# Gate/up of an fp32 encoder block: which operand of the matmul stands and which moves

## Chip, cores and metric

One NeuronCore of a Trainium2 chip runs the whole kernel in one launch. The metric is the device time of one execution in microseconds (us). A kernel is timed in several runs, and the median is given with the lowest and the highest. The profile is one further execution, taken by the hardware profiler.

TensorE (PE) multiplies: a stationary tile of 128x128 is loaded first (PEld in the profile), then a moving tile of up to 512 columns streams past it, and the sums land in PSUM, which has 8 banks of 128x512 fp32. VectorE (DVE), ScalarE (ACT) and GpSimd (POOL) do the elementwise work. SyncE (SP) issues the transfers from and to DRAM. Each engine works through its own instructions in the order in which the program lists them, and waits where a tile is not there yet or not yet free.

## Reference

An encoder block over 512 tokens of width 2048, in fp32: a projection, two attention mixers of 8 heads, an output projection with a residual, and a SwiGLU feed-forward of width 5632.

```python
mixed = jnp.concatenate([out_a, out_b], axis=-1)
x = x + jnp.einsum('bse,ed->bsd', mixed, w_out[layer])
h2 = rmsnorm(x, g_ffn[layer])
gate, up = jnp.split(jnp.einsum('bsd,df->bsf', h2, w_gate_up[layer]), 2, axis=-1)
x = x + jnp.einsum('bsf,fd->bsd', jax.nn.silu(gate) * up, w_down[layer])
return rmsnorm(x, g_final)
```

## The kernel before

**Numbers.** Each fp32 operand is split into a high part (ACT copies it rounded) and a low part (DVE subtracts the high part). `mm3` (L170) makes one product of three matmuls: high by high, high by low, low by high (L172 to L174).

**Stages on TensorE.** Input projection and attention run to about 610 us, the output projection (PSUM tiles `pw`) to 720, gate/up (`gu`) to 1610, down (`dn` plain, `st` in Strassen form) to 2036, and the last down tiles (`fd`) with the final norm to the end. The output projection has two rounds of four chunks of 512 columns, kinds A and B. After each B chunk, DVE adds the residual (L570), and `h_side` (L624) transposes two pairs of 128-row tiles of the new x (`x1t`, L629); `pair_forms` (L596) makes the forms of a pair.

**Strassen-like forms.** Gate/up multiplies 2x2 blocks in seven products, m1 to m7. On the token side `pair_forms` makes four differences of 256 columns (`ta`, `tb`, L601) and splits them, in the pieces m1, b2, ta and tb, ACT and DVE by turns. There are eight pairs, `hf[0]` to `hf[7]`, and four more for each of the three down sets. On the weight side `Form.weights` (L668) makes sums of weight blocks (`m`, L676), and `split_hi` (L698, ACT at L702) and `split_lo` (L212, DVE) give the tiles `fw`.

**Gate/up.** 44 groups (`Group`, L707), one for each f-tile of 128. A group has seven forms by two halves of the 2048 rows; each is a unit of 12 matmuls with a weight tile stationary and 256 columns of a token form moving. The result has f on the partitions. `chain_step` (L739) copies or adds the forms' results out of PSUM as soon as each is done, DVE multiplies by the norm's factor, spread over partitions by `spread_r2` (L643) into `r2b`, ACT applies silu (L764), and the product `up` is stored to DRAM as one act tile. The first group (`post`, L785) runs all forms of half 0, then all of half 1. Down reads the act tiles back.

**Order.** The program writes every engine's order by hand, over a list `units` with estimated durations. Before unit n, `prepare(n)` (L1048) issues the raw loads that are due within `LOAD_AHEAD` (24 us of estimated time) as far as one of the four raw buffers of 1 MB is free, the loads of side inputs within `SIDE_AHEAD` (13), and the high parts of weights within `SPLIT_AHEAD` (10), each low part one unit after its high part. Then the unit's matmuls follow, and one entry of the `side` queue is taken: an eviction, a transposition, a step of attention. All working tiles are slots of one pool of 80 (`N_SLOTS`).

Of the kernel before, what the change touches and what calls it, by code (L numbers as in the profile page):

```python
# [19 lines left out]
P = 128  # L20
# [23 lines left out]
LAST_WAIT = 2  # L44
PLAIN_WAIT = 5
DOWN_PLAIN = (8, 4, 4)
# [9 lines left out]
def encoder_block(ctx, tc, x, g_mix, w_in, g_q_a, g_k_a, g_out_a, g_out_b, w_out, g_ffn,  # L56
# [3 lines left out]
    wp = ctx.enter_context(tc.tile_pool(name="wstream", bufs=1))  # L60
    dp = ctx.enter_context(tc.tile_pool(name="spill", bufs=1, space=bass.MemoryType.DRAM))
    sp = ctx.enter_context(tc.tile_pool(name="slots", bufs=1))
# [10 lines left out]
    def slot(base, dtype=F32, shape=(P, 512)):  # L73
        return sp.tile(list(shape), dtype, tag="s", bufs=N_SLOTS, name=nm(base))

# [21 lines left out]
    r2b = cp.tile([P, S], F32, name="r2b")  # L97
# [60 lines left out]
    def split(src, name, gain=None, between=None):  # L158
        hi, lo = slot(name + "h", F32R), slot(name + "l", F32R)
        if gain is None:  # L160
            nc.scalar.activation(hi, src, AF.Copy)
            nc.vector.tensor_tensor(lo, src, f32(hi), op=OP.subtract)
# [18 lines left out]
    class Raw:  # L181
        def __init__(self, pieces, first=False):
            self.pieces, self.first, self.t = pieces, first, None

        def load(self):
            if self.t is None:
                self.t = wp.tile([P, 4 * 512], F32, tag="raw", bufs=N_RAW, name=nm("raw"))
# [8 lines left out]
    class Unit:  # L196
        dur = UNIT_US

        def __init__(self, raw, sub, mm, post=None, early=None, side_in=None):
            self.raw, self.sub, self.mm, self.post = raw, sub, mm, post  # L200
            self.early, self.side_in = early, side_in or []
# [15 lines left out]
    side = deque()  # L217

# [6 lines left out]
    def x_transposes(k):  # L225
# [3 lines left out]
        if k == 0:  # L229
            xT[k] = split(ps, "xT", gm[:, k:k + 1])  # L230
            nc.scalar.activation(ssx, ps, AF.Square)
        else:
            sq = slot("xsq")
            xT[k] = split(ps, "xT", gm[:, k:k + 1], lambda: nc.scalar.activation(sq, ps, AF.Square))
# [69 lines left out]
    def post_kvA(ps):  # L304
        for j in range(2):
            vA[j] = (slot("vh", F32R, (P, 2, 256)), slot("vl", F32R, (P, 2, 256)))
# [15 lines left out]
    def transpose_k_a(kv):  # L322
# [3 lines left out]
        kTA[kv] = split(ps, "kT")  # L326
# [11 lines left out]
    def post_vB(j, ps):  # L338
        for t in range(NT):
            r = r1["r"][:, t:t + 1]  # L340
            h, l = slot("vbh", F32R), slot("vbl", F32R)
# [26 lines left out]
    H = {}  # L368
    oT = {}
    acc = {}  # L370
    heads = []

    class Head:
# [126 lines left out]
    def add_chunk(w, rows, pieces, mm, post, early=None, side_in=None, dur=UNIT_US):  # L500
        for j in range(0, len(rows), 4):
# [6 lines left out]
            for s in range(m):  # L508
# [3 lines left out]
                units[-1].dur = dur  # L512

    def in_chunk(pieces, post):
# [7 lines left out]
        add_chunk(w_in, [k * P for k in range(KD)], pieces, mm, lambda: post(box["ps"]))  # L522
# [23 lines left out]
    def out_chunk(kind, c):  # L546
# [3 lines left out]
        def early(k):  # L550
            if (kind, k) not in oS:
                drain_until(lambda: (kind, k) in oT)
                oS[kind, k] = split(oT.pop((kind, k)), "oS", go[:, base + k:base + k + 1])

        def mm(u, k):
            if k == 0:
                box["ps"] = [bank("pw") for _ in range(NT)]
                if kind == "A":
                    x1[c] = [slot("x1") for _ in range(NT)]
# [5 lines left out]
        def post():  # L565
# [9 lines left out]
            if kind == "B":  # L575
# [7 lines left out]
                if c == NC - 1:  # L583
                    side.append(spread_r2)
        add_chunk(w_out, [(base + k) * P for k in range(NHA)], [(c * 512, 0, 512)], mm, post, early)
# [8 lines left out]
    m1_pair = []  # L594

    def pair_forms(a, b, kind, n):  # L596
        ta, tb = slot("ta"), slot("tb")
        left, right = slice(0, 256), slice(256, 512)
# [3 lines left out]
        if kind == "B":  # L602
            tt(ta[:, left], a[:, right], a[:, left])
            tt(tb[:, left], b[:, right], a[:, right])
            tt(ta[:, right], b[:, right], ta[:, left])
        else:
            tt(ta[:, left], a[:, right], b[:, right], OP.add)
            tt(tb[:, left], a[:, left], a[:, right])
            tt(ta[:, right], ta[:, left], a[:, left])
        tt(tb[:, right], b[:, left], ta[:, right])  # L610
        if n % 2 == 0:
            m1_pair[:] = [slot("m1h", F32R), slot("m1l", F32R)]
        m1 = cols(m1_pair, 256 * (n % 2), 256)
        nc.scalar.activation(m1[0], a[:, left], AF.Copy)
        nc.vector.tensor_tensor(m1[1], a[:, left], f32(m1[0]), op=OP.subtract)
        sb, s1, s2 = split(b, "b2"), split(ta, "ta"), split(tb, "tb")
        last = ("m3", "m4") if kind == "B" else ("m4", "m3")
        return {"m1": m1, "m2": cols(sb, 0, 256), last[0]: cols(sb, 256, 256), "m5": cols(s1, 0, 256),
                "m6": cols(s1, 256, 256), "m7": cols(s2, 0, 256), last[1]: cols(s2, 256, 256)}
# [4 lines left out]
    def h_side(i, half):  # L624
# [3 lines left out]
        for t in range(NT):  # L628
            nc.tensor.transpose(ps[:, t * P:(t + 1) * P], x1[c][t][:, j * P:(j + 1) * P], ident)  # L629
        h = hpart[half] = slot("hs")  # L630
        nc.scalar.activation(h, ps, AF.Copy, scale=gf[:, k:k + 1])
        if half == 0:
            return
        hf[i] = pair_forms(hpart.pop(0), hpart.pop(1), "B", i)
# [8 lines left out]
    def spread_r2():  # L643
        r = r2["r"]
        ps = bank("r2")
        for t in range(NT):
            nc.tensor.transpose(ps[:, t * P:(t + 1) * P], r[:, t:t + 1].to_broadcast([P, P]), ident)
        nc.scalar.activation(r2b, ps, AF.Copy)

# [6 lines left out]
    FIRST = ("m1", "m2", "m4", "m5", "m7", "m6", "m3")  # L656
    FIRST_BANK = {"m2": 0, "m3": 1, "m4": 2, "m1": 4, "m5": 5, "m6": 6, "m7": 7}
    act_dram = [dp.tile([P, 512], F32, tag=f"act{f}", name=f"act{f}") for f in range(NFF)]

    class Form(Unit):  # L660
        dur = FORM_US

        def __init__(self, raw, sums, form, half, kind, blk, mm, post):
            self.raw, self.sums, self.form, self.half, self.kind = raw, sums, form, half, kind
# [3 lines left out]
        def weights(self):  # L668
# [10 lines left out]
            def five():  # L679
                if ("m5", half) not in sums:  # L680
                    if self.kind == "A":
                        keep("m5", blk(1, 0), blk(1, 1), OP.add)
                    else:
                        keep("m5", blk(0, 1), blk(0, 0))
# [3 lines left out]
            if self.kind == "A":  # L688
                return {"m1": lambda: blk(0, 0), "m2": lambda: blk(0, 1), "m4": lambda: blk(1, 1),
                        "m7": lambda: keep("m7", blk(0, 0), blk(1, 0)),  # L690
                        "m6": lambda: keep("m6", five(), blk(0, 0)),
                        "m3": lambda: keep("m3", blk(0, 1), sums["m6", half])}[form]()
# [5 lines left out]
        def split_hi(self):  # L698
            self.src = self.weights()
            c = self.src.shape[2]  # L700
            self.w = tuple(slot("fw", F32R).rearrange("p (k c) -> p k c", c=c) for _ in range(2))
# [5 lines left out]
    class Group:  # L707
        def __init__(self, f, chain):
            self.f, self.chain, self.ps, self.st = f, chain, None, {}
            raws = [Raw(lambda t, half=half: self.pieces(t, half)) for half in range(2)]  # L710
            sums = {}

            def blk(t, i, j):
                return t.rearrange("p (k q g c) -> p k q g c", q=2, g=2, c=P)[:, :, j, i, :]

            def add(form, half, post):
# [436 lines left out]
```

## Time and profile before

| | us |
|---|---|
| median of 3 runs | 2092.77 |
| lowest and highest run | 2091.62, 2093.23 |
| profiled execution (span) | 2088.0 |
| gate/up on TensorE (first to last `gu` matmul) | 720.8 to 1609.8 |

The profile's page gives each engine's busy time and share, the chain of work that ended last, and groups of instructions by source line, written `line engine operation out<-in shape xcount | busy us, mean ns | idle time before them and what ended it`. A timeline row is `start us, duration us, engine, line, operation, out<-in, count`, with a wait in brackets. A matmul's duration there includes the pipeline; how fast matmuls follow each other is read from their starts. A table of stretches gives busy time by engine between two moments.

### The profile page before, as it was taken

The page shows a single profiled execution, that of the slowest core. Times are in us where ns is not written, and L with a number is a line of the kernel's source. Part 1 is how long each engine was busy: PE and PEld are TensorE (multiplying, and loading weights), DVE is VectorE, ACT ScalarE, POOL GpSimd, SP SyncE. Part 2 cuts the span into 40 slices and gives each one's busy share as a digit, 9 for nine tenths or more (in the row PEclk, how much of TensorE's full clock was granted, in tenths as well). Part 3 has the DMA queues.
Part 4 walks back from the last instruction along what each step waited for, and adds up shares of the span by engine and source line. Part 5 has one row for each costly group of instructions (what it writes and reads, how often), then busy time and mean ns, then how long its engine had stood idle before and what let it go on. Part 6 is the DMA issues. An engine that isn't in the chain of part 4 may idle for free.

```text
span 2088.0 us, 35761 instructions
## 1 busy us (share of the span) xinstructions
PE 2074.9 (99%) x14363; PEld 1933.4 (93%) x14363; DVE 1502.8 (72%) x2794; ACT 965.1 (46%) x1889; POOL 56.5 (3%) x53
## 2 busy tenths in 40 slices
PE   9999999999999999999999999999999999999998
PEld 7888888888888899999999999999999999999997
DVE  6555755555645797878788787887878957869876
ACT  5334344444443655444454444444445534435443
POOL 3100100000000000000000000000000000000000
PEclk9999999999999999999999999999999999999999
DMA  7222211212324444453544534444355444234342
GB/s 247 101 87 75 81 61 61 81 61 82 120 101 139 124 112 122 107 137 97 132 116 113 136 98 132 110 118 130 99 136 174 154 166 148 66 117 142 103 161 81
DMA packets 274406, 241.67 MB, mean 116 GB/s; under 512 B 7568, under 2 KB 212928, under 8 KB 274240
## 3 DMA queue, kind: packets, MB, share of 16 engines
q1 hardware_dynamic: 274064, 239.32, 37.6%
q8 instruction: 112, 1.84, 0.4%
q14 instruction: 54, 0.44, 0.1%
q10 hardware_dynamic: 176, 0.07, 0.0%
HBM read 219.44 MB, written 19.92 MB: 115 GB/s over the span
## 4 chain that ended last, share of the span: by engine, by line
PE 97%; DVE 2%; issue 1%; ACT 0%; DMA 0%; ACTq 0%; POOLq 0%; POOL 0%; DVEq 0%
PE gu L172 14%; PE gu L174 14%; PE gu L173 14%; PE pj L173 6%; PE pj L174 6%; PE pj L172 6%; PE st L173 6%; PE st L174 6%; PE st L172 6%; PE pw L172 3%; PE pw L174 3%; PE pw L173 3%; PE pt L421 1%; PE o L172 1%; PE o L174 1%
## 5 line engine op out<-in xcount | busy, mean ns | idle before, releaser
L702 ACT ACTIVATE fw<-m 128x512 fp32r<-128x512 f32 x448 | 280.1, 626 | 358.1 <-DVE m L676 337.9
L212 DVE TENSOR_TENSOR fw<-m,fw 128x512 fp32r<-128x512 f32 x448 | 307.8, 687 | 99.4 <-ACT fw L702 61.0
L212 DVE TENSOR_TENSOR fw<-raw,fw 128x512 fp32r<-128x512 f32 x336 | 226.0, 685 | 54.0 <-ACT fw L702 42.7
L172 PE MATMUL pj<-wh,xTh 128*128 128x512 f32 x576 | 228.1, 396 | 0.0
L173 PE MATMUL pj<-wl,xTh 128*128 128x512 f32 x576 | 225.0, 391 | 0.4 <-DVE wl L212 0.4
L174 PE MATMUL pj<-wh,xTl 128*128 128x512 f32 x576 | 225.2, 391 | 0.0
L212 DVE TENSOR_TENSOR wl<-raw,wh 128x512 fp32r<-128x512 f32 x288 | 203.5, 727 | 10.7 <-ACT wh L207 8.8
L702 ACT ACTIVATE fw<-raw 128x512 fp32r<-128x512 f32 x336 | 197.4, 620 | 10.6 <-PE st L173 10.6
L172 PE MATMUL gu<-tah,fw 128*128 128x256 f32 x704 | 199.8, 284 | 0.0
L172 PE MATMUL gu<-b2h,fw 128*128 128x256 f32 x704 | 199.6, 284 | 0.0
L172 PE MATMUL gu<-tbh,fw 128*128 128x256 f32 x704 | 199.6, 284 | 0.0
L174 PE MATMUL gu<-tbh,fw 128*128 128x256 f32 x704 | 199.6, 283 | 0.0
L174 PE MATMUL gu<-tah,fw 128*128 128x256 f32 x704 | 199.5, 283 | 0.0
L174 PE MATMUL gu<-b2h,fw 128*128 128x256 f32 x704 | 199.5, 283 | 0.0
L173 PE MATMUL gu<-b2l,fw 128*128 128x256 f32 x704 | 199.5, 283 | 0.0
L173 PE MATMUL gu<-tbl,fw 128*128 128x256 f32 x704 | 199.5, 283 | 0.0
L173 PE MATMUL gu<-tal,fw 128*128 128x256 f32 x704 | 199.5, 283 | 0.0
L207 ACT ACTIVATE wh<-raw 128x512 fp32r<-128x512 f32 x288 | 169.6, 626 | 12.3 <-PE pj L174 4.3
L676 DVE TENSOR_TENSOR m<-raw 128x512 f32<-128x512 f32 x224 | 153.3, 684 | 2.1 <-PE st L173 2.0
L172 PEld LDWEIGHTS gu<-tah,fw 128*128 128x128 f32 x704 | 135.2, 192 | 0.2 <-ACT uw L750 0.2
L172 PEld LDWEIGHTS gu<-b2h,fw 128*128 128x128 f32 x704 | 135.3, 192 | 0.0
L172 PEld LDWEIGHTS gu<-tbh,fw 128*128 128x128 f32 x704 | 135.3, 192 | 0.0
(252 smaller groups left out, 5420.9 us busy)
## 6 DMA issues: line engine op xcount, KB each, us to landing
raw<-in_w_gate_up_dram SPq DMA_DIRECT2D x176, 512.0 KB, 5.5
raw<-in_w_down_dram SPq DMA_DIRECT2D x44, 1024.0 KB, 5.2
raw<-in_w_in_dram SPq DMA_DIRECT2D x19, 1024.0 KB, 4.9
raw<-in_w_in_dram SPq DMA_DIRECT2D x32, 512.0 KB, 4.3
raw<-in_w_out_dram SPq DMA_DIRECT2D x16, 1024.0 KB, 5.1
act<-up SPq DMA_DIRECT2D x44, 256.0 KB, 2.0
actf<-act SPq DMA_DIRECT2D x44, 256.0 KB, 5.3
x<-in_x_dram SPq DMA_DIRECT2D x32, 256.0 KB, 5.5
```

Of the source, the lines that this page charges most:

```text
L172: nc.tensor.matmul(dst, ah, bh, start=start, stop=False, skip_group_check=chained)
L173: nc.tensor.matmul(dst, ah, bl, start=False, stop=False, skip_group_check=chained)
L174: nc.tensor.matmul(dst, al, bh, start=False, stop=stop, skip_group_check=chained)
L207: nc.scalar.activation(self.w[0], src, AF.Copy)
L212: nc.vector.tensor_tensor(self.w[1], self.src, f32(self.w[0]), op=OP.subtract)
L421: nc.tensor.transpose(ps[:, t * P:(t + 1) * P], self.p[t][:, kb * P:(kb + 1) * P], ident)
L676: nc.vector.tensor_tensor(d, a, b, op=op)
L702: nc.scalar.activation(self.w[0], self.src, AF.Copy)
```

## The change

Gate/up is turned round. Eleven `ColBlock`s of four f-tiles take the place of the 44 groups. A unit (`Cols`) is one form of one pair: two token tiles of 128x128 of the form are stationary, and 512 weight columns move, in six matmuls. A block has 7 x 8 = 56 units. The result has tokens on the partitions, so silu takes the norm's factor as a scale per row, `spread_r2` and `r2b` go, and at the end of a block `turn` transposes the four act tiles on TensorE, ACT copies them out of PSUM, and SP stores them. Evictions are no longer queued in `side` but tied to unit numbers (`hooks`). Weight blocks are loaded in pieces of 128x512 (256 KB) as each form needs them, several of them more than once: 56 loads a block.

`pair_forms` makes its differences in one tile of 8 x 256 columns, then takes one ACT copy and one DVE subtraction of 1792 columns. The forms of the eight pairs lie in fixed tiles (`arena`), which before gate/up serve as homes of attention's operands and some weights (`home`). The outputs of 13 heads are stored to DRAM by ACT's queue and read back before the output projection (`Back`). Split weights outside gate/up go through rings of 12 tiles (`wslot`), the raw budget there is three buffers of 1 MB instead of four, in gate/up four, counted in words. A pair of act tiles is read back in four transfers of 128 KB instead of two of 256 KB.

```diff
+COLS_AHEAD = 7.0
+COLS_US = 1.37
...
+SPILL_B = 5
+COL_TILES = 14
+W_TILES = {"wi": 12, "wo": 12, "wd": 12, "wf": 12, "wl": 32}
...
+    def wslot(tag):
+        if tag == "wa":
+            ring[0] += 1
+            return home(16 + ring[0] % 12)
+        return sp.tile([P, 512], F32R, tag=tag, bufs=W_TILES[tag], name=nm("w"))
...
+    arena = [sp.tile([P, 7 * 512], F32, tag="arena", bufs=8, name=f"arena{i}") for i in range(8)]
+
+    def home(n, dtype=F32R, shape=(P, 512)):
+        ap = arena[n // 7][:, n % 7 * 512:(n % 7 + 1) * 512].bitcast(dtype)
+        return ap if len(shape) == 2 else ap.rearrange("p (a b) -> p a b", a=shape[1])
...
-            self.src, self.w = src, (slot("wh", F32R), slot("wl", F32R))
+            self.src, self.w = src, (wslot(self.tag), wslot(self.tag))
...
+            if self.kind == "A" or self.h < SPILL_B:
+                nc.scalar.dma_start(o_dram[self.kind, self.h], o)
...
+        class Back:
+            def __init__(self, k):
+                self.k = k
+
+            def load(self):
+                drain_until(lambda: (kind, self.k) in oT)
+                self.t = slot("oback")
+                nc.sync.dma_start(self.t, o_dram[kind, self.k])
+
+            def split(self):
+                oS[kind, self.k] = split(self.t, "oS", go[:, base + self.k:base + self.k + 1],
+                                         at=2 * self.k + (0 if kind == "A" else 42))
...
-    m1_pair = []
-
-    def pair_forms(a, b, kind, n):
-        ta, tb = slot("ta"), slot("tb")
-        left, right = slice(0, 256), slice(256, 512)
+    ORDER = ("m1", "m2", "m4", "m5", "m6", "m7", "m3")
+
+    def pair_forms(w, dst):
+        def part(n):
+            return w[:, n * 256:(n + 1) * 256]
+        a_r, a_l, b_l, b_r, s1, s2, s3, s4 = (part(n) for n in range(8))
 
         def tt(out, x, y, op=OP.subtract):
             nc.vector.tensor_tensor(out, x, y, op=op)
...
+        tt(s1, a_r, b_r, OP.add)
+        tt(s3, a_l, a_r)
+        tt(s2, s1, a_l)
+        tt(s4, b_l, s2)
+        hi, lo = dst[:, :7 * 256].bitcast(F32R), dst[:, 7 * 256:].bitcast(F32R)
+        nc.scalar.activation(hi, w[:, 256:], AF.Copy)
+        nc.vector.tensor_tensor(lo, w[:, 256:], f32(hi), op=OP.subtract)
+        return {form: cols((hi, lo), n * 256, 256) for n, form in enumerate(ORDER)}
...
+        for n, t in enumerate((2, 3, 0, 1) if half == 0 else range(NT)):
+            nc.tensor.transpose(ps[:, n * P:(n + 1) * P], x1[c][t][:, j * P:(j + 1) * P], ident)
         if half == 0:
-            return
-        hf[i] = pair_forms(hpart.pop(0), hpart.pop(1), "B", i)
+            hpart[0] = sp.tile([P, 4 * 512], F32, tag="pair", bufs=2, name=nm("pair"))
+        nc.scalar.activation(hpart[0][:, half * 512:(half + 1) * 512], ps, AF.Copy, scale=gf[:, k:k + 1])
+        if half == 1:
+            hf[i] = pair_forms(hpart.pop(0), arena[i])
...
-    def spread_r2():
...
+    class Cols(Unit):
+        ahead = COLS_AHEAD
+        dur = COLS_US
+
+        def __init__(self, box, form, i, raws):
+            self.box, self.form, self.i, self.raws = box, form, i, raws
+            self.post, self.early, self.side_in = None, None, []
+
+        def split_hi(self):
+            self.src = self.box.weights(self.form, self.i, *[r.t for r in self.raws])
+            self.w = tuple(sp.tile([P, 512], F32R, tag="cw", bufs=COL_TILES, name=nm("cw")) for _ in range(2))
+            nc.scalar.activation(self.w[0], self.src, AF.Copy)
 
         def mm(self, u):
...
+            self.box.multiply(self)
...
+    class ColBlock:
+        def __init__(self, w, lo, pairs, forms):
+            self.pairs, self.forms = pairs, forms
+            self.ps, self.sums = {}, {}
+            self.begin = len(units)
+
+            def raw(i, j, q):
+                row = (2 * q + i) * P
+                return Raw(lambda t: [(w[0, row:row + P, lo[j]:lo[j] + 512], t)], width=512)
+            b00 = [raw(0, 0, q) for q in range(pairs)]
+            b10 = [raw(1, 0, q) for q in range(pairs)]
+            for form in CHAIN:
+                for q in range(pairs):
+                    raws = {"m1": lambda: [b00[q]], "m7": lambda: [raw(1, 1, q), raw(0, 1, q)],
+                            "m6": lambda: [b00[q]], "m2": lambda: [b10[q]],
+                            "m5": lambda: [raw(0, 1, q), raw(0, 0, q)], "m4": lambda: [b10[q]],
+                            "m3": lambda: [raw(1, 1, q)]}[form]()
+                    units.append(Cols(self, form, q, raws))
+
+        def weights(self, form, q, *t):
+            if form in ("m1", "m2", "m3"):
+                return t[0]
+            a, b, op = {"m7": lambda: (t[0], t[1], OP.subtract), "m6": lambda: (self.sums["m7", q], t[0], OP.add),
+                        "m5": lambda: (t[0], t[1], OP.subtract),
+                        "m4": lambda: (t[0], self.sums["m6", q], OP.subtract)}[form]()
+            d = self.sums[form, q] = slot("sum")
+            nc.vector.tensor_tensor(d, a, b, op=op)
+            return d
+
+        def bank_of(self, form):
+            name = CHAIN_BANK[form]
+            if name not in self.ps:
+                self.ps[name] = [bank(name + "c") for _ in range(2)]
+            return self.ps[name]
+
+        def multiply(self, u):
+            drain_until(lambda: self.forms[u.i] is not None)
+            dst = self.bank_of(u.form)
+            for t in range(2):
+                mm3(dst[t], cols(self.forms[u.i][u.form], t * P), u.w, u.form in ("m1", "m7", "m2") and u.i == 0,
+                    u.i == self.pairs - 1, True)
+
+        def after(self, form, late, f):
+            hook(self.begin + (CHAIN.index(form) + 1) * self.pairs - 1 + late, f)
+
+    def gate_up_block(f0):
+        box = ColBlock(w_gate_up, (f0 * P, DFF + f0 * P), KD // 2, hf)
+        st = {}
+
+        def tile2(name):
+            st[name] = slot(name, F32, (P, 2, 512))
+            return st[name]
+
+        def snap(form, name):
+            def go():
+                d = tile2(name)
+                for t in range(2):
+                    nc.scalar.activation(d[:, t], box.bank_of(form)[t], AF.Copy)
+            box.after(form, 0, go)
+
+        def add(form, late, src, name):
+            def go():
+                d = tile2(name)
+                for t in range(2):
+                    nc.vector.tensor_tensor(d[:, t], box.bank_of(form)[t], st[src][:, t], op=OP.add)
+            box.after(form, late, go)
+
+        def silu(form, late, name, half):
+            def go():
+                for t in range(2):
+                    nc.scalar.activation(st[name][:, t], st[name][:, t], AF.Silu,
+                                         scale=r2["r"][:, 2 * half + t:2 * half + t + 1])
+            box.after(form, late, go)
+
+        def low():
+            for t in range(2):
+                nc.vector.tensor_tensor(st["glo"][:, t], box.bank_of("m3")[t], st["glo"][:, t], op=OP.mult)
+
+        def high():
+            nc.vector.tensor_tensor(st["uhi"], st["uhi"], st["ghi"], op=OP.mult)
+
+        def turn(k):
+            ps = bank("at")
+            for t in range(NT):
+                src = st[("glo", "uhi")[t // 2]][:, t % 2, k * P:(k + 1) * P]
+                nc.tensor.transpose(ps[:, t * P:(t + 1) * P], src, ident)
+            a = slot("actT")
+            nc.scalar.activation(a, ps, AF.Copy)
+            nc.sync.dma_start(act_dram[f0 + k], a)
+        snap("m1", "s1")
+        snap("m7", "s7")
+        snap("m6", "s6")
+        add("m2", 1, "s1", "glo")
+        silu("m2", 4, "glo", 0)
+        add("m5", 1, "s7", "uhi")
+        add("m4", 1, "s6", "ghi")
+        silu("m4", 4, "ghi", 1)
+        box.after("m3", 1, low)
+        box.after("m3", 3, high)
+        for k in range(4):
+            box.after("m3", 8 + 2 * k, lambda k=k: turn(k))
+
+    gu_begin = len(units)
+    for f in range(0, NFF, 4):
+        gate_up_block(f)
...
-            self.t = [slot("actf") for _ in range(2)]
-            for i in range(2):
-                nc.sync.dma_start(self.t[i], act_dram[self.f + i])
+            self.t = sp.tile([P, 4 * 512], F32, tag="pair", bufs=2, name=nm("pair"))
+            for dst, src, lo in ((0, 0, 256), (256, 0, 0), (512, 1, 0), (768, 1, 256)):
+                nc.sync.dma_start(self.t[:, dst:dst + 256], act_dram[self.f + src][:, lo:lo + 256])
 
         def split(self):
-            self.forms[self.n] = pair_forms(*self.t, "A", self.n)
+            self.forms[self.n] = pair_forms(self.t, sp.tile([P, 7 * 512], F32, tag="forms", name=nm("forms")))
...
-        last_use[u.raw] = n
+        for r in u.raws:
+            last_use[r] = n
     live = []
 
     def load_raws(n):
-        while done["load"] < len(units) and at[done["load"]] <= at[n] + LOAD_AHEAD:
-            raw = units[done["load"]].raw
-            if raw.t is None:
-                live[:] = [r for r in live if last_use[r] >= done["lo"]]
-                if len(live) == N_RAW:
-                    return
-                live.append(raw)
-                raw.load()
+        while done["load"] < len(units) and at[done["load"]] <= at[n] + units[done["load"]].load_ahead:
+            for raw in units[done["load"]].raws:
+                if raw.t is None:
+                    live[:] = [r for r in live if last_use[r] >= done["lo"]]
+                    if sum(r.width for r in live) + raw.width > (RAW_WORDS if gu_begin <= done["load"] < down_begin else PLAIN_RAW_WORDS):
+                        return
+                    live.append(raw)
+                    raw.load()
...
-        while done["hi"] < len(units) and at[done["hi"]] <= at[n] + SPLIT_AHEAD:
+        while done["hi"] < len(units) and at[done["hi"]] <= at[n] + units[done["hi"]].ahead:
...
+        for f in hooks.pop(n, ()):
+            f()
...
-N_RAW = 4
+RAW_WORDS = 4 * 2048
+PLAIN_RAW_WORDS = 3 * 2048
```

More of the change, by code (lines that the diff above doesn't have):

```diff
@@ L366, in post_qkB @@
             push_head(("B", 2 * j + h))
-    H = {}
     oT = {}
+    o_dram = {(g, h): dp.tile([P, 512], F32, tag=f"o{g}{h}", name=f"o{g}{h}")
+              for g, n in (("A", NHA), ("B", SPILL_B)) for h in range(n)}
     acc = {}
@@ L902, in strassen_chunk @@
             for h in range(2):
-                units.append(Form(raws[h], sums, form, h, "B", blk, mm, (lambda form=form: step(form)) if h else None))
+                units.append(Form(raws[h], sums, form, h, blk, mm, (lambda form=form: step(form)) if h else None))
         def plain_mm(u, i):
```

200 lines of the change are left out of this document (38 added, 162 removed).

## Prediction

> **What bounds the kernel now.** I read the page first (its span, the busy shares, the chain of waits), then the table of stretches that I cut at the stages, then TensorE's waits.
>
> ```profile
> span 2088.0 us, 35761 instructions
> ...
> PE 2074.9 (99%) x14363; PEld 1933.4 (93%) x14363; DVE 1502.8 (72%) x2794; ACT 965.1 (46%) x1889; POOL 56.5 (3%) x53
> ...
> PE 97%; DVE 2%; issue 1%; ACT 0%; DMA 0%; ACTq 0%; POOLq 0%; POOL 0%; DVEq 0%
> ```
> ```profile
> 610.00:720.00 110.00, 109.36 (x505) 90.10 (x503) 65.09 (x117) 50.97 (x104) 0.00 (x0) 1.00 0.38 124
> 720.50:1609.90 889.40, 889.22 (x7410) 889.05 (x7411) 724.02 (x1259) 440.29 (x857) 1.38 (x1) 1.00 0.44 120
> 1609.90:2036.00 426.10, 424.17 (x3361) 415.89 (x3360) 330.53 (x589) 193.89 (x351) 0.00 (x0) 1.00 0.40 137
> ```
> ```profile
> PE dn L173 <- DVE wl L212: 1.9, 2, 1.0
> ```
> Columns of the second fence: stretch and length, then busy time of PE, weight load, DVE, ACT, POOL, then clock, DMA share, GB/s. TensorE works all the time in the out projection, in gate/up and down, at clock 1.00; DVE is at 81% in gate/up (724.02 of 889.40). Nearly nothing is waited for: the row of the third fence is TensorE's largest wait (1.9 us in total, two times, the longest 1.0). So the time falls only with TensorE's own work, and any new wait is added in full. The profiled span is 2088.0 us, the median of the runs 2092.77: I carry the sum against the span and add 4.8 at the end.
>
> **1. Matmuls of gate/up.** The cadence comes from TensorE's timeline, one stretch with 256 moving columns and one with 512:
>
> ```profile
> 739.72 0.28 PE L174 MATMUL gu<-tbh,fw 128*128 128x256 f32 x1
> ...
> 743.92 0.28 PE L173 MATMUL gu<-m1l,fw 128*128 128x256 f32 x1
> ```
> ```profile
> 299.74 0.39 PE L172 MATMUL pj<-wh,xTh 128*128 128x512 f32 x1
> ...
> 303.60 0.39 PE L174 MATMUL pj<-wh,xTl 128*128 128x512 f32 x1
> ...
> 304.51 0.60 PE L421 MATMUL pt<-ident,p 128*128 128x128 f32 x4
> 304.86 0.48 PE L172 MATMUL pj<-wh,xTh 128*128 128x512 f32 x1
> 305.18 0.39 PE L173 MATMUL pj<-wl,xTh 128*128 128x512 f32 x1
> 305.41 0.40 PE L174 MATMUL pj<-wh,xTl 128*128 128x512 f32 x1
> 305.65 0.39 PE L172 MATMUL pj<-wh,xTh 128*128 128x512 f32 x1
> ```
> 35 intervals of 256 columns take 4.20 us (0.120 each), 17 of 512 columns take 3.86 (0.227). Before: 44 groups of 168, 7392 x 0.120 = 887.0 (the stretch: 889.2 with 18 other instructions). After: 11 blocks of 56 units of 6, 3696 x 0.2267 = 837.9. **-49.1.** The two cadences are one line: 0.1067 per 256 columns and 0.0133 per matmul, and half as many matmuls pay the latter.
>
> A rule that speaks against it: the Trainium skill, "TensorE: Matmul & The Clock Gate", section "Wait — 56ns, not 53.3ns?", puts the fixed part of a back-to-back matmul at about 2.5 ns. By it the halving would save an estimated 3696 x 2.5 ns = 9.2 us; the column part agrees with the rows here, the fixed part does not (13.3 ns).
>
> **2. Transposes of the results.** 44 new groups of four 128x128. One costs what stands above: 304.51 to 304.86 is 0.35, and the next interval is 0.32 instead of 0.227, 0.44 together. **+19.5**, and -0.4 for the removed `spread_r2` group. So TensorE's own work falls by 30.0. A gain below that needs waits.
>
> **3. A gate/up block in its steady part.** Engines' prices, by form and from back-to-back rows:
>
> ```profile
> L702 ACT ACTIVATE fw<-m 128x512 fp32r<-128x512 f32 x448 | 280.1, 626 | 358.1 <-DVE m L676 337.9 <-PE st L173 19.1 <-PE dn L173 0.5
> ...
> L746 ACT ACTIVATE uv<-gu 128x256 f32<-128x256 f32 x43 | 16.5, 383 | 25.0 <-PE gu L174 25.0
> ```
> ```profile
> L212 DVE TENSOR_TENSOR fw<-m,fw 128x512 fp32r<-128x512 f32 x448 | 307.8, 687 | 99.4 <-ACT fw L702 61.0 <-PE st L173 26.4 <-PE st L174 10.0
> ...
> L752 DVE TENSOR_TENSOR gg<-gu,uv 128x256 f32<-128x256 f32 x43 | 18.3, 425 | 51.4 <-PE gu L174 51.4
> ```
> ```profile
> 708.61 0.43 DVE L601 TENSOR_TENSOR tb<-hs,hs 128x256 f32<-128x256 f32 x1 [1.49 <-ACT hs L631]
> ...
> 711.28 0.68 DVE L162 TENSOR_TENSOR tbl<-tb,tbh 128x512 fp32r<-128x512 f32 x1
> 711.88 1.28 DVE L212 TENSOR_TENSOR wl<-raw,wh 128x512 fp32r<-128x512 f32 x2
> ```
> DVE starts a 512-column operation every 0.60 us. A block has 56 low parts, 32 sums of weights, 8 evictions, and one product of 1024: 96 x 0.60 + 1.2 = 59 us, beside 336 x 0.2267 + 4 x 0.44 = 77.9 on TensorE, 76% (81% before). ACT has 56 high parts, 6 copies, 4 silus, 4 copies of transposed results: 70 x 0.63 = 44 us. The heavy forms (m7, m6, m5, m4) want two DVE operations per unit, 1.21 us, against 6 x 0.2267 = 1.36. Averages fit; what decides is the order. By the order of the changed kernel, weights are prepared mostly 30 to 50 matmuls (7 to 11 us) ahead, 14 to 20 in the first block, and the tightest reload (end of m5) is issued 36 matmuls, 8.2 us, ahead of its use. Between lie a landing, a sum and two splits (0.68 + 0.63 + 0.69 = 2.0).
>
> ```profile
> act<-up SPq DMA_DIRECT2D x44, 256.0 KB, 2.0
> actf<-act SPq DMA_DIRECT2D x44, 256.0 KB, 5.3
> ```
> ```profile
> GB/s 0 88 365 314 341 346 329 345 389 386 388 353 293 290 130 82 310 393 382 343 334 343 257 135 334 394 334 298 361 386 66 238 405 176 0 0 0 0 6 0
> ```
> A 256 KB transfer takes 2.0 (a store) to 5.3 us (a read with others in flight): 8.2 - 2.0 - 5.3 = 0.9 us left at the worst. 56 loads of 256 KB and the 1 MB of results are 15.7 MB in 77.9 us, 202 GB/s, against 120 before; the second fence, the first 52 us in 40 slices, shows 300 to 400 GB/s sustained. I take **0**; bounds 0 and +35 (rival B).
>
> A rule that speaks against it: the Trainium skill, "DMA: Bandwidth & Descriptors", section "Bandwidth", advises batches of 1 MiB. Between its 64 KB (0.95 us) and 1 MB (6.15 us) rows a 256 KB load is an estimated 2.0 us; taken one at a time a block would need 112 us. The slices above, with 256 KB loads of x among them, show several in flight, so the rows here do not bear that out; it stands under B as its extreme.
>
> **4. `pair_forms` as one lump.** Before, ACT and DVE work by turns on pieces. After: four differences, one ACT copy of 1792 columns, one DVE subtraction of 1792, and DVE, in order, waits for ACT. The trace has no such width; from 256 and 512 columns above, ACT 0.63 + 5 x 0.243 = 1.84, DVE 0.69 + 5 x 0.262 = 2.00, differences 4 x 0.36 = 1.46: 5.3 to 5.4 us of DVE, against 3.6 before (the first and the next row, of DVE's timeline at the exit):
>
> ```profile
> 1602.62 0.42 DVE L601 TENSOR_TENSOR ta<-actf,actf 128x256 f32<-128x256 f32 x1
> ...
> 1606.23 0.68 DVE L212 TENSOR_TENSOR wl<-raw,wh 128x512 fp32r<-128x512 f32 x1
> ```
> Queued behind it on DVE are the low parts of the next weights, and TensorE waits for those. There are 20 pairs, in four places.
>
> Out projection, six pairs. In the chain of waits:
>
> ```profile
> 707.41 0.45 PE x1t L629 x4
> 707.88 0.70 ACT hs L631
> ```
> The next low part was ready at 711.88 + 0.69, 5.2 us after 707.41; now 1.2 + 5.4 + 0.7 = 7.3 to 7.5. By the order TensorE needs it after 27 matmuls (6.1) or 31 (7.0): 1.4 and 0.5 late, three times each. **+5.7** (0 to 11).
>
> Entry to gate/up. The last two pairs follow the last `x1t` groups. The old first group ran the seven forms of pairs 0 to 3 first; now m1 wants pair 7 in its eighth unit: after 7 units and four transpose groups, 7 x 1.36 + 1.8 = 11.3 us from the first, while two pairs in a row, 2 x 6.5, and five low parts between, 3.0, take 16. **+5.2** (2 to 8).
>
> Exit to down, first set: eight plain units with four pairs. Two units ask DVE for four low parts and a pair, 2.4 + 5.4 = 7.8 us, and TensorE for 24 x 0.2267 = 5.44: 2.4 short per pair. The first pair is early; walking the order gives 8.75 of the 9.4, against 2.25 now (the 1.9 above and the pipeline's refill). **+6.5** (0 to 9).
>
> Sets two and three: the last pair stands ahead of a plain unit's low part, 2.3 late each; **+4.7** (0 to 9). With three 1 MB buffers in place of four outside gate/up, one reload per set is near late: **+1**.
>
> **5. Spilled heads.** 13 stores on ACT's queue and 13 reads back on SP's: about 0.45 us of issue each, at most 5.9 on the path; ACT is at 46% of the span, I take **+1.5**.
>
> Sum: -49.1 + 19.5 - 0.4 + 0 + 5.7 + 5.2 + 6.5 + 4.7 + 1 + 1.5 = -5.4; span 2082.6, time **2087.3**. With the lumps at two thirds to one and a half of that, 2080 to 2100.
>
> **The rivals.** *A: the lumps are hidden.* If the low parts have more lead than I counted, only TensorE's -30.0 is left: 2088.0 - 30 + 4.8 = 2063, or 2068 with the exit alone. For it: a low part is waited for twice only in the whole trace of before (the row of `dn`). Against: those two stand behind just such a lump, at 3.6 us.
>
> *B: the weights of gate/up come late* (slower). In m7 and m5 each unit takes two fresh 256 KB loads, 512 KB per 1.36 us, 385 GB/s, as much as the best slices above; half of the 16 can be ahead. At the mean of those slices, some 300, eight loads need 7.0 us where 5.4 are given: 1.6 us late per heavy form, 22 forms, +35, time 2122. It decides from a landing of over 6 us. The same place would show it if DVE, at 89% there, fell behind an eviction. Its extreme, one load at a time at the store's 2.0 us, makes a block 112 us instead of 77.9, time 2460; the slices leave that under 0.01. For B: the smallest margin is 0.9 us, and 11 blocks repeat it. Against: the loads queue early and m6 and m4 load nothing.
>
> *C: the price of 512 columns is not that of the projection.* Behind a transpose group the rows above show 0.235 (305.18 to 305.65); at that in all of gate/up the gain shrinks by 31, time 2118. The Trainium skill's fixed 2.5 ns (its page and section in step 1) would shrink it by 40, an estimate.
>
> *D: the change evens out.* The lumps cost half as much again, or each block 0.7 us at its seam: 2090 to 2097.
>
> **How the numbers follow.** Chances: forecast (2078 to 2089) 0.30, A 0.18, D 0.21, B 0.27, C 0.04. Under about 0.2% (4.2 us) a measurement of this kernel cannot tell from no change. Faster is A and the forecast, 0.48; within it D, 0.21; slower B and C, 0.31. The likeliest case's own range is 2078 to 2093; for 8 in 10, from most of A (2066) to most of B (2114).
>
> **What would show it.** `gu`-like matmuls 0.227 apart and 3696 of them; gaps of 0.44 for a transpose group; waits of TensorE on DVE's low parts only in the out projection, at the entry and at the exit, of 1 to 6 us; a gate/up stage of about 860 to 865 us. Wrong if the waits there name a raw tile or a sum of weights (B), or if the waits at the four places add up to less than 10 us (A).

## The result and the profile after

The changed kernel takes 2109.09 us (median of 4 runs, 2107.95 to 2110.76), the kernel before 2092.19 beside it: 1.0084 times the time, 95% interval 1.0070 to 1.0098. It is slower by 17 us; 5 to 6 faster was forecast. The profiled execution has a span of 2107.7, against 2088.0.

The page of the changed kernel, its span and its busy times; then the stretches of the changed kernel, cut at its own stages (out projection, gate/up, down; columns as before):

```profile
span 2107.7 us, 29650 instructions
...
PE 2065.2 (98%) x10839; PEld 1764.3 (84%) x10839; DVE 1456.7 (69%) x2566; ACT 985.4 (47%) x1765; POOL 56.3 (3%) x53
```
```profile
610.00:728.70 118.70, 115.92 (x531) 94.14 (x529) 64.31 (x99) 54.80 (x93) 1.40 (x1) 1.00 0.41 138
730.00:1595.90 865.90, 861.91 (x3871) 712.28 (x3870) 680.99 (x1083) 460.79 (x778) 1.31 (x1) 1.00 0.61 201
1595.90:2056.00 460.10, 437.14 (x3379) 423.66 (x3378) 330.36 (x558) 191.91 (x324) 0.00 (x0) 0.98 0.38 129
```

Gate/up fell from 888.9 to 865.7 us, as the change meant. The rest more than gave it back. From the first and last matmul of each stage in the two traces:

| stage on TensorE | before | after | difference |
|---|---|---|---|
| to the first gate/up matmul | 720.8 | 730.0 | +9.2 |
| gate/up | 888.9 | 865.7 | -23.2 |
| down, to the first `fd` matmul | 426.4 | 460.2 | +33.8 |
| from there to the end | 51.9 | 51.7 | -0.2 |

So 34 of the 43 us that were lost lie in down, a stage whose products the change does not touch. TensorE's waits in the changed kernel, largest first (total us, times, longest):

```profile
PE dn L190 <- DVE w L232: 11.8, 7, 3.5
PE st L189 <- ACT s L903: 9.2, 6, 2.7
PE zc L190 <- DVE cw L232: 2.9, 2, 2.8
PE pw L190 <- DVE w L232: 2.8, 6, 0.7
PE st L190 <- DVE w L232: 1.9, 2, 1.4
```

Before, the first of these rows was 1.9 and the others did not exist. `zc`, a bank of gate/up, waits twice, both in the first block: its 2.9 us, and 1.1 more on ACT, are the entry. The other ten blocks wait for nothing.

A third loss stands in no list of waits. TensorE's timeline behind the long wait at the entry, whole rows one after another:

```profile
746.06 0.80 PE L190 MATMUL zc<-cw,arena 128*128 128x512 f32 x1 [2.76 <-DVE cw L232]
746.65 0.63 PE L191 MATMUL zc<-cw,arena 128*128 128x512 f32 x1
747.08 0.63 PE L189 MATMUL zc<-cw,arena 128*128 128x512 f32 x1
```

The starts are 0.43 apart instead of 0.227, up to 750.92: TensorE runs at half its clock there. Stretches cut behind that wait and behind one in down have a granted clock (third column from the end) of 0.50:

```profile
746.10:751.30 5.20, 5.20 (x12) 4.09 (x13) 4.19 (x8) 2.49 (x6) 0.00 (x0) 0.50 0.97 319
1612.60:1618.00 5.40, 5.40 (x13) 4.24 (x14) 4.29 (x8) 1.68 (x2) 0.00 (x0) 0.50 0.00 0
```

Each matmul of 512 columns costs 0.20 us more in such a stretch; 2.6 us were lost behind the entry's wait and 5.9 behind the three long waits on `dn` in down, added up over the matmuls' starts. (Counted over the starts, a wait comes out some 0.2 us longer than in its row, which counts from the modelled end of a matmul.) "TensorE: Matmul & The Clock Gate" of the Trainium skill, section "Why this matters for your kernels", warns of idle gaps above some 3 us between bursts of matmuls. This trace agrees for its waits of 3.0 to 3.6 us by the starts, which all have the clock at 0.50 behind them. But one of 2.6 us (from 1789.5) has 0.53 over the next 3 us, and one of 2.7 us (from 1954.5) has 1.00. The length alone does not decide it; that is taken up under the fifth kernel below.

### The profile page after: what moved, and what is told of

Its sections match the earlier page's. It is cut to its first block, busy times and chain, and to the rows that moved or that the text cites. A ratio compares the mean times of both kernels' runs of the same rounds, so it can differ in the third digit from the quotient of the medians.

```text
span 2107.7 us, 29650 instructions
## 1 busy us (share of the span) xinstructions
PE 2065.2 (98%) x10839; PEld 1764.3 (84%) x10839; DVE 1456.7 (69%) x2566; ACT 985.4 (47%) x1765; POOL 56.3 (3%) x53
## 5 line engine op out<-in xcount | busy, mean ns | idle before, releaser
L734 ACT ACTIVATE cw<-sum 128x512 fp32r<-128x512 f32 x352 | 221.3, 633 | 260.7 <-DVE sum L765 179.0
L190 PE MATMUL zc<-cw,arena 128*128 128x512 f32 x704 | 274.6, 390 | 2.9 <-DVE cw L232 2.9
L189 PE MATMUL zc<-cw,arena 128*128 128x512 f32 x704 | 274.6, 390 | 1.1 <-ACT arena L649 1.1
L191 PE MATMUL zc<-cw,arena 128*128 128x512 f32 x704 | 274.4, 390 | 0.0
L232 DVE TENSOR_TENSOR cw<-sum,cw 128x512 fp32r<-128x512 f32 x352 | 241.1, 685 | 40.7 <-ACT cw L734 11.9
L232 DVE TENSOR_TENSOR w<-raw,w 128x512 fp32r<-128x512 f32 x328 | 229.5, 720 | 52.0 <-ACT w L718 26.2
L232 DVE TENSOR_TENSOR cw<-raw,cw 128x512 fp32r<-128x512 f32 x264 | 171.8, 687 | 97.4 <-ACT cw L734 66.2
L189 PE MATMUL pj<-w,arena 128*128 128x512 f32 x576 | 229.3, 398 | 1.2 <-ACT w L227 1.2
L190 PE MATMUL pj<-w,arena 128*128 128x512 f32 x576 | 225.1, 391 | 0.9 <-DVE w L232 0.9
L191 PE MATMUL pj<-w,arena 128*128 128x512 f32 x576 | 225.8, 392 | 0.1
L189 PE MATMUL st<-w,forms 128*128 128x256 f32 x672 | 191.8, 285 | 9.2 <-ACT s L903 9.2
L734 ACT ACTIVATE cw<-raw 128x512 fp32r<-128x512 f32 x264 | 153.2, 624 | 81.5 <-PE zc L191 32.3
L190 PE MATMUL st<-w,forms 128*128 128x256 f32 x672 | 190.9, 284 | 0.0
L191 PE MATMUL st<-w,forms 128*128 128x256 f32 x672 | 190.8, 284 | 0.0
L190 PEld LDWEIGHTS zc<-cw,arena 128*128 128x128 f32 x704 | 132.4, 188 | 30.9 <-DVE cw L232 3.7
L189 PEld LDWEIGHTS zc<-cw,arena 128*128 128x128 f32 x704 | 132.3, 188 | 28.9 <-ACT arena L649 1.5
L191 PEld LDWEIGHTS zc<-cw,arena 128*128 128x128 f32 x704 | 132.4, 188 | 27.5
L189 PE MATMUL yc<-cw,arena 128*128 128x512 f32 x352 | 141.6, 402 | 0.0
L191 PE MATMUL yc<-cw,arena 128*128 128x512 f32 x352 | 138.1, 392 | 0.0
L190 PE MATMUL yc<-cw,arena 128*128 128x512 f32 x352 | 137.7, 391 | 0.0
```

What stands on the lines that cost most here:

```text
L189: nc.tensor.matmul(dst, ah, bh, start=start, stop=False, skip_group_check=chained)
L190: nc.tensor.matmul(dst, ah, bl, start=False, stop=False, skip_group_check=chained)
L191: nc.tensor.matmul(dst, al, bh, start=False, stop=stop, skip_group_check=chained)
L232: nc.vector.tensor_tensor(self.w[1], self.src, f32(self.w[0]), op=OP.subtract)
L734: nc.scalar.activation(self.w[0], self.src, AF.Copy)
```

## The experiments

Three places had to be told apart: the lump in `pair_forms`, the raw buffers in down, and the start, where TensorE was already 4.2 us behind at 20 us. All kernels below compute the whole block. Kernels that ran together share 7 to 21 runs of the kernel before, median 2091.6.

### The lump in two pieces (2087.84 us)

```diff
+        hi, lo = dst[:, :7 * 256].bitcast(F32R), dst[:, 7 * 256:].bitcast(F32R)
+        nc.scalar.activation(hi[:, :768], w[:, 256:1024], AF.Copy)
         tt(s1, a_r, b_r, OP.add)
...
-        hi, lo = dst[:, :7 * 256].bitcast(F32R), dst[:, 7 * 256:].bitcast(F32R)
-        nc.scalar.activation(hi, w[:, 256:], AF.Copy)
-        nc.vector.tensor_tensor(lo, w[:, 256:], f32(hi), op=OP.subtract)
+        nc.scalar.activation(hi[:, 768:], w[:, 1024:], AF.Copy)
+        nc.vector.tensor_tensor(lo[:, :768], w[:, 256:1024], f32(hi[:, :768]), op=OP.subtract)
+        nc.vector.tensor_tensor(lo[:, 768:], w[:, 1024:], f32(hi[:, 768:]), op=OP.subtract)
```

> One edit to the changed kernel: pair_forms converts in two pieces. ACT copies the 768 columns that need no difference while DVE makes the differences, then the 1024 of the differences; DVE subtracts 768, then 1024. DVE no longer idles 1.77 us inside a pair, so a pair takes about 3.9 us of DVE instead of 5.35. Theory L (the idle DVE inside the lump holds up the next weights' low parts, and each long wait also halves the clock for the matmuls behind it): the waits of plain down matmuls on low parts fall from 11.8 to 4 us or less, those of the out projection from 2.8 to about 0, the long wait at the entry from 2.8 to about 1, and the stretches at clock 0.50 behind them (together some 9 us lost) mostly go: 14 to 20 us faster than the changed kernel, 2089 to 2095. Rival Q (what is late is ACT's queue or DVE's plain sum of work, not the idle inside the lump): less than 5 us faster, 2104 or more, and the waits stay above 8 us.

Measured 2087.84 (11 runs), 21.3 faster than the changed kernel and 0.9983 of the kernel before (0.9975 to 0.9992). DVE's timeline at the exit to down, first in the changed kernel, then with two pieces:

```profile
1597.53 1.55 DVE L643 TENSOR_TENSOR pair<-pair 128x256 f32<-128x256 f32 x4
1600.84 2.03 DVE L650 TENSOR_TENSOR forms<-pair,forms 128x1792 fp32r<-128x1792 f32 x1 [1.77 <-ACT forms L649]
1602.79 0.68 DVE L232 TENSOR_TENSOR w<-raw,w 128x512 fp32r<-128x512 f32 x1
```
```profile
1593.31 1.55 DVE L643 TENSOR_TENSOR pair<-pair 128x256 f32<-128x256 f32 x4
1594.78 0.95 DVE L651 TENSOR_TENSOR forms<-pair,forms 128x768 fp32r<-128x768 f32 x1
1595.99 1.23 DVE L652 TENSOR_TENSOR forms<-pair,forms 128x1024 fp32r<-128x1024 f32 x1 [0.26 <-ACT forms L650]
1597.14 0.69 DVE L232 TENSOR_TENSOR w<-raw,w 128x512 fp32r<-128x512 f32 x1
```

A pair takes 3.83 us up to the next low part instead of 5.26: DVE's idle 1.77 us inside it shrank to 0.26. The waits on low parts followed:

```profile
PE st L189 <- ACT s L905: 10.2, 6, 2.6
PE dn L190 <- DVE w L232: 6.5, 5, 2.0
PE zc L190 <- DVE cw L232: 1.6, 1, 1.6
```

`dn` went from 11.8 to 6.5, the out projection's row is gone, and no wait on a low part in gate/up or in a plain unit was followed by a lower clock: the longest is now 2.0. By stages of the profiled executions, 4.8 us came before gate/up, 5.4 in it, 11.7 in down. Theory L holds, with a little more gained than the 14 to 20 us expected, and with more left on `dn` than the 4 us. The waits on ACT's evictions did not move, so they have another cause.

### Four raw buffers in down again (2094.02 us)

```diff
-                    if sum(r.width for r in live) + raw.width > (RAW_WORDS if gu_begin <= done["load"] < down_begin else PLAIN_RAW_WORDS):
+                    if sum(r.width for r in live) + raw.width > (RAW_WORDS if gu_begin <= done["load"] else PLAIN_RAW_WORDS):
```

> One edit to the changed kernel: four raw buffers of 1 MB in down again instead of three (still three ahead of gate/up). Theory R (the Strassen chunks of down wait because ACT stands still in front of a raw tile whose load was issued too late, behind the third buffer): TensorE's waits in the Strassen chunks, 9.2 us on ACT's evictions and 1.9 on low parts, fall to 2 or less, 8 to 12 us faster than the changed kernel, 2097 to 2101. Rival S (the load is late because SP stands in front of the act stores and the x loads, whatever the buffers): under 3 us faster, and ACT still waits 5.9 us for a raw tile there.

What made theory R: in the changed kernel ACT stood still in front of a raw tile, and the eviction of a full PSUM bank stood behind it. SP's queue, then ACT's timeline:

```profile
1641.59 2.06 SPq L211 DMA_DIRECT2D raw<-in_w_down_dram  x2
```
```profile
1646.87 0.63 ACT L718 ACTIVATE w<-raw 128x512 fp32r<-128x512 f32 x1 [5.92 <-DMA raw<-in_w_down_dram]
...
1647.92 0.58 ACT L903 ACTIVATE s<-st 128x512 f32<-128x512 f32 x1
```

Measured 2094.02 (11 runs), 15.1 faster than the changed kernel, some 3 more than expected. With four buffers the waits are:

```profile
PE dn L190 <- DVE w L232: 8.8, 6, 3.1
PE st L189 <- ACT s L903: 3.0, 2, 1.7
...
PE st L190 <- DVE w L232: 1.4, 1, 1.4
```

The Strassen chunks wait 4.4 us instead of 11.1 (2 or less was expected), and `dn` gained 3.0 too. ACT's waits for a raw tile in down, first in the changed kernel, then with four buffers:

```profile
ACT w L718 <- DMA raw<-in_w_down_dram: 38.4, 12, 5.9
```
```profile
ACT w L718 <- DMA raw<-in_w_down_dram: 2.1, 2, 1.4
```

R holds: it was the buffer, not SP's queue.

### The x tiles apart (2109.24 us)

```diff
+    xall = sp.tile([P, 7, NT, P], F32, tag="xall", name="xall")
...
-        xs[k] = slot(f"x{k}", F32, (P, NT, P))
+        xs[k] = xall[:, k] if k < 7 else slot(f"x{k}", F32, (P, NT, P))
```

> One edit to the changed kernel: the first seven x tiles lie in one tile of their own, so that no load of x waits for a reader of another tile's place. Theory X (the 4.2 us lost in the first 17 us come from the fourth x load, which waits for the gains' transposition whose place it shares, and from the fifth, which waits for the first x tile to be read): the shift of TensorE at 20 us falls from 4.2 to 1 or less and the time by 3 to 4.2, 2105 to 2106. Rival Y (transfers at the start just land at other moments from execution to execution): the shift is of any size and the time within 1 us of the changed kernel.

The tile pool of the changed kernel chooses the places itself, and it put the fourth x tile where the gains' tile lies (SP's waits name the gains' transfer there, 1.1 us). On SP's queue that load leaves at 5.25 us in the changed kernel, and at 3.82 with the tiles apart (and before the change):

```profile
5.25 0.38 SPq L99 DMA_DIRECT2D x<-in_x_dram  x1
```
```profile
3.82 0.44 SPq L100 DMA_DIRECT2D xall<-in_x_dram  x1
```

TensorE works 4.00 of the four us from 10 to 14 instead of 1.90, and reaches the same matmul at 25.0 us instead of 27.2 (23.0 before the change). So the mechanism is there, at half the size expected in this execution. Why only half stands in TensorE's first matmuls, here and then with all three edits, where the same matmul comes at 23.2:

```profile
8.12 0.63 PE L192 MATMUL pj<-w,arena 128*128 128x512 f32 x1
8.55 0.63 PE L190 MATMUL pj<-w,arena 128*128 128x512 f32 x1
```
```profile
7.03 0.39 PE L192 MATMUL pj<-w,arena 128*128 128x512 f32 x1
7.26 0.40 PE L190 MATMUL pj<-w,arena 128*128 128x512 f32 x1
```

In the first execution TensorE starts at half its clock, 0.43 us a matmul up to 10.68; in the second it has its full clock from the first of these matmuls on, as in the profiles of the changed kernel and of the kernel before. That takes back about 2 us of what the tiles gave. What decides how an execution starts is not shown.

The time is the same within 0.2 us: the profile shows 2.1 us still gained at the end of the out projection and 2.9 at the end of gate/up, and all but 0.4 of it gone in down, a stage that came out 2.6 us longer. Alone, the edit is worth nothing that these runs can tell.

### The three together (2070.08 us)

> The three edits together. If L, R and X hold and their places are apart: the sum, 25 to 36 us faster than the changed kernel, 2073 to 2084, that is 8 to 19 us faster than the kernel before. If a freed wait only moves to the next resource (DVE's sum of work in the down sets, where 7.8 us of low parts and pairs stand against 5.4 of TensorE for two units): 15 us or less, 2094 or more.

Measured 2070.08 (4 runs), 0.9900 of the kernel before (0.9885 to 0.9915) and 39 faster than the changed kernel, a little over the range expected. This version beats both. What is left of TensorE's waits, the two largest:

```profile
PE dn L191 <- DVE w L233: 4.8, 2, 3.2
PE st L190 <- ACT s L906: 1.6, 1, 1.6
```

Gate/up takes 860.3 us here, from 721.5 to 1581.7, and down 433.8, still 7.4 above before.

### Two pieces and four buffers, without the x tiles (2072.81 us)

> Two pieces and four raw buffers in down, without the x tiles apart. If the two effects are independent: 2109.1 - 21.3 - 15.1 = 2072.7, and the x tiles are worth the rest to 2070.1, some 2.6 us, which the x tiles alone did not show (0.1 us). If they overlap, 2077 or more.

2072.81 (4 runs): the two gains add up to a tenth of a microsecond, and with both edits in place the x tiles are worth 2.7 us.

This kernel and the three together have the same longest wait on `dn`, 3.2 us at the exit, but only this one loses clock behind it. Wherever the clock halves between the first matmuls and the final norm in the ten traces, it does so for 3.41 us or twice that. Cut into pieces of this length, the stretches at the wait are as follows, first here, then with the three edits (first numbers: length, PE busy; third from the end: clock):

```profile
1597.49:1600.91 3.42, 0.50 (x2) 0.46 (x3) 3.17 (x4) 2.56 (x4) 0.00 (x0) 1.00 1.06 383
1600.91:1604.32 3.41, 3.41 (x9) 2.65 (x9) 3.39 (x7) 1.36 (x2) 0.00 (x0) 0.50 0.65 239
```
```profile
1591.62:1595.03 3.41, 1.61 (x8) 0.99 (x6) 3.12 (x7) 1.92 (x4) 0.00 (x0) 1.00 1.08 371
1595.03:1598.45 3.42, 2.01 (x9) 1.66 (x10) 3.42 (x5) 1.95 (x5) 0.00 (x0) 1.00 1.05 387
1598.45:1601.86 3.41, 3.41 (x17) 2.77 (x15) 3.18 (x7) 1.50 (x3) 0.00 (x0) 1.00 0.18 65
```

Here the wait fills most of one piece, and the next piece has half the clock. There it straddles two, and none has. No run moved a wait by itself to test that this is the reason; what all traces say of it stands at the end.

### The low part ahead of the pair (2070.66 us, and 2109.88 with the lump)

```diff
             for v in self.side_in:
-                v.split()
+                if type(v).__name__ != "Pair":
+                    v.split()

         def split_lo(self):
             nc.vector.tensor_tensor(self.w[1], self.src, f32(self.w[0]), op=OP.subtract)
+            for v in self.side_in:
+                if type(v).__name__ == "Pair":
+                    v.split()
```

> The three edits together and one more: where a plain unit of down carries a pair, its own low part stands ahead of the pair on DVE, not behind it. Theory O (at the exit the order on DVE makes the wait: the low part is ready only after 3.9 us of pair): the two waits of 3.2 and 1.6 us on low parts at the exit fall to 1 or less together, 3 to 5 us faster than the three edits alone, 2065 to 2067. Rival H (the low part waits for its high part, whose ACT instruction waited 2.75 us for TensorE to release a tile's place): within 1 us of 2070.

> The changed kernel with that order alone; the pair stays one lump of 5.35 us and down has three raw buffers. Theory O: the waits of down's plain units on low parts fall from 11.8 to 5 us or less, with one or two of the half-clock stretches of some 2 us behind them, 8 to 12 us faster than the changed kernel, 2097 to 2101; the out projection and the entry to gate/up stay as they are. Rival: the next unit's low part is late instead, by about as much, under 4 us gained, 2105 or more.

Neither gained. On top of the three edits 2070.66 stands against 2070.08, on the changed kernel alone 2109.88 against 2109.09. The waits moved. First the two rows with the lump, in down:

```profile
PE st L189 <- ACT s L907: 16.9, 11, 3.5
PE dn L190 <- DVE w L233: 6.0, 3, 3.1
```
```profile
PE dn L191 <- DVE w L234: 2.5, 2, 2.1
PE st L190 <- ACT s L910: 2.4, 2, 1.3
```

With the lump, `dn` fell by 5.8 and the evictions rose by 7.7. On top of the three edits `dn` fell by 2.3, but down, 433.7 against 433.8, stayed as long. TensorE's rows say where the gain went:

```profile
1597.87 0.79 PE L191 MATMUL dn<-w,acth 128*128 128x512 f32 x1 [2.12 <-DVE w L234]
1598.47 0.63 PE L192 MATMUL dn<-w,actl 128*128 128x512 f32 x1
1598.89 0.63 PE L190 MATMUL dn<-w,acth 128*128 128x512 f32 x1
```

Behind the shorter wait, 2.1 us, the clock was halved up to 1601, some 1.4 us lost that the longer one had not cost; and in a Strassen chunk (start 1619.12) TensorE waited another 1.3 us, for an eviction of ACT. The rivals' times were nearer. That DVE's sum of work is short at the exit, and the order only says who waits, fits the moved waits but was not tested by itself. That ACT's high part is what is late (rival H) was not shown: it still waited 3.2 us for TensorE there, yet the low part was waited for less.

### Gate/up with twelve places instead of sixteen (2186.01 us)

```diff
-RAW_WORDS = 4 * 2048
+RAW_WORDS = 3 * 2048
```

> The changed kernel with 12 places of 256 KB for gate/up weights instead of 16. Eight are held from m1 to m6, so m7 and m5 turn over four. If the loads of gate/up have little margin (my rival B): a place is free again after landing, 4.3 us, and a sum, 0.7, for two units of 2.7 us of TensorE, so most of m7 and m5 runs at the loads' pace: 50 to 200 us slower than the changed kernel. If the lead of 24 us of estimated time is what counts and the places are not: less than 10 us slower.

2186.01 (2 runs), 77 slower than the changed kernel. The new row is the bank of m7, where two fresh loads a unit are wanted:

```profile
PE yc L190 <- DVE cw L232: 45.9, 15, 4.6
```

Gate/up took 938.4 us, 72.7 more: these waits, and a granted clock of 0.97 over the stage. Rival B of the prediction is real with a quarter less room. At sixteen places it does not decide.

## Why the prediction was wrong, and where it was right

**Steps 1 to 3 were right.** In gate/up of the changed kernel matmuls follow at the cadence of the projection (first and last of a stretch of its timeline, 18 intervals in 4.08 us, 0.227), and a transpose group costs what was worked out: 0.36 to the next matmul, then 0.31 in place of 0.227, 0.44:

```profile
899.74 0.39 PE L191 MATMUL zc<-cw,arena 128*128 128x512 f32 x1
...
903.82 0.39 PE L191 MATMUL zc<-cw,arena 128*128 128x512 f32 x1
```
```profile
825.96 0.38 PE L824 MATMUL at<-ident,glo 128*128 128x128 f32 x2
...
826.32 0.47 PE L189 MATMUL yc<-cw,arena 128*128 128x512 f32 x1
826.63 0.39 PE L190 MATMUL yc<-cw,arena 128*128 128x512 f32 x1
```

Rival C did not come. Nor did the smaller saving by the fixed 2.5 ns per matmul of the Trainium skill ("TensorE: Matmul & The Clock Gate", section "Wait — 56ns, not 53.3ns?"): 0.227 less twice the prediction's 0.1067 leaves 13 ns again. Steady gate/up waits for nothing, at 201 GB/s where 202 was worked out, so rival B did not come either, though 2109 lies among its times; with the three edits the stage is 28.6 us shorter than before.

**Step 4 was right about the lump.** ACT's copy of 1792 columns takes 1.70 us (1.84 estimated), DVE's subtraction 2.03 (2.00), a pair 5.26 (5.3 to 5.4). Counted over TensorE's starts, the out projection lost 4.0 us for 5.7, the entry 4.6 for 5.2 (the prediction's own 16 less 11.3 is 4.7), the plain units of down 13.0 where 2.25 were lost before, so 10.7 for 6.5 + 4.7.

**The step that failed first is the +1 for three raw buffers in place of four.** I costed one reload per set as nearly late for its own weights. What the late tile held up was ACT, which stood in front of it with the PSUM evictions of a Strassen chunk behind, and TensorE waited for the bank: 9.2 us on evictions and 1.9 on low parts in these chunks, a place that the prediction's list of waits does not have. Four buffers took 6.7 us of these 11.1 away and gave 15.1 us back in all, with the waits on `dn` and the clock behind both.

**The second is what the sum lacked: the clock behind a wait.** Each stall was priced by its length, as if the clock of 1.00 in the table of stretches stayed. Four of them were followed by matmuls of 512 columns at half the clock, 8.5 us in all, beside 12.7 us for those four waits themselves; a stretch of `st` from 1648.7 (clock 0.57 over 3 us) adds an estimated 1.3.

**The third is the start**, for which the sum had no term: 4.2 us in the profiled execution. TensorE waited 1.2 and 0.9 us there for parts of weights, and the clock behind was 0.60 from 13.4 to 17.0. With the tiles apart both are gone; most of what was left of the delay in that execution, 2.0 us, was its start at half the clock. In the rest of the input projection and in attention the trace drifts by another 1 us, for which +1.5 was put down to the spilled heads.

So the sum of 24.6 us of losses became 49.7 (the span's +19.7 against TensorE's -30.0). By the starts, the lumps cost 19.3 for 22.1, the Strassen waits 12.4 for 1, the clock 10 and the start 4 for nothing, the drift 1 for 1.5; some 3 us are not assigned.

## What to carry to other kernels

When a change joins short operations of two engines into one long one, count the time in which the second engine stands idle in between, and ask who waits behind it: here 1.5 us an instance, in 20 instances, cost 21 us with the clock behind the waits. When a buffer is taken away, look at what stands in the in-order queue behind the instruction that will wait for it; the late tile's own user is not the one that pays. On an engine with no slack, price a wait by its length and by what the clock does after it: here up to some 3 us more, and nothing where the wait happened to straddle two of its pieces of 3.41 us.

## What had not been expected of the hardware

The clock after a wait goes by more than the wait's length. Over the profiles of the changed kernel and of the first four experiments, thirteen waits of TensorE of 1.7 to 1.9 us, counted over the starts, were never followed by a lower clock. Of twenty between 2.05 and 3.65 us seventeen were, at a granted clock of 0.50 to 0.73 over the next 3 us, and three were not (2.2, 2.7 and 3.4 us). So a stall that grows from 1.8 to 2.6 us can cost twice its growth, or more. What separates them in these traces is where the wait falls. Cut all ten traces into the pieces of 3.41 us in which the clock changes and look at the pieces at full clock, without the last 45 us: none in which TensorE stood idle for up to 0.50 of the piece was followed by half the clock, all with 0.54 or more were, and in between there are both. That is a count over these traces, not an experiment.
